# Weight blocks split by DMA: the high part rounded by the loading DMA, the low part accumulated onto its negative

## The chip, the cores and the metric

The kernel runs on one core of one Trainium2 chip. The metric is the device time of one execution in microseconds. Beside the runs that are timed, one execution is profiled; its trace gives the durations used here.

## What is computed

One layer of a hybrid model over 512 tokens of width 2048, in float32. A projection of the input feeds three mixers (retention, mLSTM, an S5 state space with a gated linear unit); their outputs, side by side, go through an output projection, a layer norm, a feed-forward with a squared ReLU, a gate and a second layer norm:

```python
mix = jnp.matmul(jnp.concatenate([y_ret, y_m, y_s], -1), w_out)
x = layer_norm(ALPHA * x + mix, ln1_w, ln1_b)

ff = jnp.matmul(jnp.square(jax.nn.relu(jnp.matmul(x, w_up))), w_down)
r = ALPHA * x + ff
ple = jax.nn.sigmoid(jnp.matmul(r, w_gate)) * jnp.matmul(p_l, w_ple)
return layer_norm(r + ple, ln2_w, ln2_b)
```

`w_up` is 2048 x 8192, `w_down` 8192 x 2048, `w_out` and `w_gate` are 2048 x 2048, `w_ple` is 256 x 2048.

## The kernel before

Activations lie feature-major: a tile of 128 features by 512 tokens. TensorE multiplies in float32r, a float32 with a rounded mantissa. To keep the accuracy of float32, each operand is split into a high part (rounded to float32r) and a low part (the rest), and each product is three matmuls: high by high, high by low, low by high (`mm3`, lines 140 to 143).

All weights are packed on the host into blocks of 128 x 1024 floats (512 KB), in the order in which they are used: W_SU, W_GATE, W_HEAD, W_GLU, then W_OUT (32 blocks), W_PLE (4), W_UP (128), W_DOWN (128) and W_G (32). `wblk` (line 129) fetches one: SP's queue loads it into a tile of the pool with tag "raw" (4 buffers), ScalarE copies it into `wh` (pool "wh", 3 buffers), which rounds it, and VectorE subtracts, `wl = raw - wh` (pool "wl", 3 buffers). These steps have a high priority, so that the scheduler of the program places them early.

The stages from W_OUT on:

- *Output projection.* For 8 groups of two output tiles, 4 blocks each; a block is 24 matmuls of 512 columns.
- *Layer norm and the small projection.* The 16 tiles x1 are normed and split while the 4 blocks of W_PLE are multiplied; the results go to memory.
- *Up and down.* 16 chunks of 512 hidden features. In a chunk, `down` forms seven products for each of two halves (a Strassen scheme with 7 instead of 8), each with a block of W_DOWN or a sum of such blocks; `up` makes the hidden features of the next chunk from 8 blocks of W_UP. Blocks and products alternate: block, product, product, block, and so on. `product` (line 1017) splits its block into `wh` and `wl` of the same two pools as `wblk`, with the same two instructions; its raw blocks have a pool of their own ("rawd").
- *Gate.* 8 groups with 4 blocks of W_G each. Groups 0 to 3 run at full width; groups 4 to 7 run twice, for the first and the second 256 tokens, and load their blocks twice, so that the second layer norm of the first half runs beside the second half's matmuls. So W_G stands for 48 calls of `wblk`.

The pool "wh" and the pool "wl" hand out their buffers in turn, in program order; who takes one waits until TensorE has read what it held before. In the earlier stages POOL's queue carries the S5 part's transfers (lines 400, 401, 478, 567, 568); from the output projection on it has no transfer, and only a third of the last layer norm's tiles (line 114).

Of the kernel before, what the change touches and what calls it, by code (L numbers as in the profile page):

```python
# [10 lines left out]
F32R = mybir.dt.float32r  # L11
# [3 lines left out]
MUL, ADD, SUB, MAX, MIN = ALU.mult, ALU.add, ALU.subtract, ALU.max, ALU.min  # L15
# [58 lines left out]
W_OUT = W_GLU + 2  # L74
# [8 lines left out]
def hybrid_block_kernel(ctx: ExitStack, tc: tile.TileContext, xT, pT, pos, wall, vec, cst, s5b, s5c, out):  # L83
    nc = tc.nc
    V, A, G, P = nc.vector, nc.scalar, nc.gpsimd, nc.tensor

    def pool(name, bufs=1, **kw):
        return ctx.enter_context(tc.tile_pool(name=name, bufs=bufs, **kw))
# [3 lines left out]
    wrp = pool("wr", 4)  # L92
    whp = pool("wh", 3)
    wlp = pool("wl", 3)
# [27 lines left out]
    def acp(out, in_, scale=1.0):  # L122
        return A.activation(out=out, in_=in_, func=AF.Copy, scale=scale)  # L123

    def split(x, hi, lo):
        acp(hi, x)
        pools["dve"] = V.tensor_tensor(out=lo, in0=x, in1=hi, op=SUB).ins  # L127

    def wblk(i, parts=1):
        with tc.high_priority(2000):  # L130
            raw = wrp.tile([128, 1024], F32, tag="raw", name="raw")
            wh = whp.tile([128, 1024], F32R, tag="wh", name="wh")
            wl = wlp.tile([128, 1024], F32R, tag="wl", name="wl")
            for p in range(parts):
                sl = slice(p * 1024 // parts, (p + 1) * 1024 // parts)
                nc.sync.dma_start(out=raw[:, sl], in_=wall[i][:, sl])
                split(raw[:, sl], wh[:, sl], wl[:, sl])
        return wh, wl
# [21 lines left out]
    def gemm(i, banks, acts, m, kb, n=None, sl=slice(0, S)):  # L160
        n = n or KT
        for b in range(n // kb):
            if i == W_SU:
                xload(2 * b)
            wh, wl = wblk(i + b, 2 if i + b == W_SU else 1)
            if i == W_SU:
                xload(2 * b + 1)
            js, qs = range(m), range(kb)
            for j, q in [(j, q) for j in js for q in qs] if n == kb else [(j, q) for q in qs for j in js]:
                k, w = b * kb + q, slice((q * m + j) * 128, (q * m + j + 1) * 128)  # L170
                xh, xl = (a[:, sl] for a in acts[k])
                mm3(banks[j], wh[:, w], wl[:, w], xh, xl, k == 0, k == n - 1)
            tick()
# [745 lines left out]
    for gidx in range(8):  # L919
        tag = ("mm", "bu")[gidx % 2]  # L920
# [18 lines left out]
    for k in range(2):  # L939
        xr = tmp("xr")  # L940
        nc.scalar.dma_start(out=xr, in_=pT[k])
        ph, pl_ = (hfp.tile([128, S], F32R, tag="h" + n, name="p" + n) for n in "hl")
# [28 lines left out]
    def up(c, g, hs):  # L971

        b = [bank("mm"), bank("mm")]
        for i in range(4):
            wh, wl = wblk(W_UP + (2 * c + g) * 4 + i)
            for q in range(4):
                for j in range(2):
                    k, w = 4 * i + q, slice((2 * q + j) * 128, (2 * q + j + 1) * 128)
                    mm3(b[j], wh[:, w], wl[:, w], *x1[k], k == 0, k == KT - 1)
            if i < 3:  # L980
                yield
        for j in range(2):
            r = ffp.tile([128, S], F32, tag="r", bufs=4, name="r")
            with tc.high_priority(400):
                A.activation(out=r, in_=b[j], func=AF.Relu)
                A.activation(out=r, in_=r, func=AF.Square)
            hs.append(r)
        yield
# [135 lines left out]
    def gate_blocks(g, b, i0, i1, sl):  # L1124
        for i in range(i0, i1):
            wh, wl = wblk(W_G + g * 4 + i)
            for q in range(4):
                for j in range(2):
                    k, w = 4 * i + q, slice((2 * q + j) * 128, (2 * q + j + 1) * 128)
                    xh, xl = (a[:, sl] for a in rr[k])  # L1130
                    mm3(b[j], wh[:, w], wl[:, w], xh, xl, k == 0, k == KT - 1)
# [157 lines left out]
```

## Time and profile before

| | |
|---|---|
| median of 3 runs | 2452.59 us (2451.07 to 2454.1) |
| the profiled execution, its own time | 2449.43 us |
| its span, first to last instruction | 2447.6 us |
| mean granted TensorE clock | 0.993 |
| TensorE matmuls busy | 2395.9 us (98%) |
| VectorE, ScalarE, POOL busy | 1816.7, 978.9, 89.4 us |
| transfers | 288.87 MB, mean 118 GB/s |

The stages by time from the span's start: heads until about 660 us, output projection until about 855, layer norm and small projection until about 905, up and down until about 2215, gate until about 2420 (half width from about 2325), the last layer norm to the end. A busy share is an average; what an engine's work is worth is seen in the stretch in which another engine waits for it.

### The profile page before, as it was taken

To read this page: it belongs to the slowest core of one execution; us is meant where nothing else is said; L and a number is where in the kernel's file an instruction comes from. 1 tells how busy PE (TensorE), PEld (TensorE's weight loads), DVE (VectorE), ACT (ScalarE), POOL (GpSimd) and SP (SyncE) were. 2 spreads that over 40 slices of the span, in tenths; PEclk is the share of its full clock that TensorE was granted. 3 is DMA by queue.
4 is the path that set the end of the run, shared out by engine and by line. 5 is a ranking of instruction groups with operands and counts; after the bars stand their busy time and mean duration, and the time that the engine had idled before them with its cause. 6 is when DMAs were issued, how large, how long until landed. Compare 5 with 4: busy or idle time off the path is not lost.

```text
span 2447.6 us, 29501 instructions
## 1 busy us (share of the span) xinstructions
PE 2395.9 (98%) x11123; PEld 1985.3 (81%) x11123; DVE 1816.7 (74%) x2904; ACT 978.9 (40%) x1379; POOL 89.4 (4%) x182
## 2 busy tenths in 40 slices
PE   9999999999999989999999999999999999988996
PEld 7888888888888868888888888888888888867896
DVE  6788989897654476767776777677767776787777
ACT  4544444444432263333433343333334343433354
POOL 4100000000000000000000000000000000000002
PEclk9999999999999999999999999999999999999998
DMA  6433333333443372333333332423242324233464
GB/s 233 146 105 102 110 110 113 113 95 106 155 151 116 117 242 94 100 107 96 111 94 113 93 113 83 124 86 121 78 129 85 117 83 122 85 104 112 129 188 141
DMA packets 99230, 288.87 MB, mean 118 GB/s; under 512 B 11744, under 2 KB 20368, under 8 KB 99088
## 3 DMA queue, kind: packets, MB, share of 16 engines
q1 hardware_dynamic: 85360, 265.49, 34.5%
q10 hardware_dynamic: 8352, 13.11, 1.6%
q0 software_dynamic: 5376, 8.39, 1.3%
q8 instruction: 87, 1.43, 0.2%
q14 instruction: 55, 0.45, 0.1%
HBM read 268.31 MB, written 18.64 MB: 117 GB/s over the span
## 4 chain that ended last, share of the span: by engine, by line
PE 93%; DVE 3%; DMA 1%; issue 1%; ACT 1%; POOL 0%; ACTq 0%; SPq 0%; DVEq 0%
PE mm L141 18%; PE mm L142 18%; PE mm L143 18%; PE wk L1031 13%; PE bu L1031 7%; PE ya L1031 5%; PE bu L142 2%; PE bu L141 2%; PE bu L143 2%; DMA pldr<-t 1%; DVE wl L127 1%; ACT wh L123 1%; PE wk L143 1%; PE wk L142 1%; PE wk L141 1%
## 5 line engine op out<-in xcount | busy, mean ns | idle before, releaser
L123 ACT ACTIVATE wh<-raw 128x1024 fp32r<-128x1024 f32 (+1 forms) x321 | 338.9, 1056 | 739.2 <-PE mm L142 500.7
L127 DVE TENSOR_TENSOR wl<-raw,wh 128x1024 fp32r<-128x1024 f32 (+1 forms) x321 | 391.4, 1219 | 276.0 <-ACT wh L123 267.6
L127 DVE TENSOR_TENSOR wl<-rawd,wh 128x1024 fp32r<-128x1024 f32 x224 | 274.1, 1224 | 179.1 <-ACT wh L123 177.1
L141 PE MATMUL mm<-x1h,wh 128*128 128x512 f32 x1024 | 398.4, 391 | 4.7 <-ACT x1h L123 2.2
L142 PE MATMUL mm<-x1l,wh 128*128 128x512 f32 x1024 | 399.9, 391 | 0.6 <-DVE x1l L127 0.6
L143 PE MATMUL mm<-x1h,wl 128*128 128x512 f32 x1024 | 399.4, 390 | 0.0
L123 ACT ACTIVATE wh<-rawd 128x1024 fp32r<-128x1024 f32 x224 | 237.3, 1060 | 305.5 <-PE wk L1031 210.0
L141 PE MATMUL mm<-xh,wh 128*128 128x512 f32 x800 | 317.4, 397 | 5.3 <-ACT wh L123 5.3
L143 PE MATMUL mm<-xh,wl 128*128 128x512 f32 x800 | 313.1, 391 | 0.0
L142 PE MATMUL mm<-xl,wh 128*128 128x512 f32 x800 | 312.3, 390 | 0.0
L141 PEld LDWEIGHTS mm<-x1h,wh 128*128 128x128 f32 x1024 | 192.3, 188 | 47.8 <-ACT x1h L123 3.5
L142 PEld LDWEIGHTS mm<-x1l,wh 128*128 128x128 f32 x1024 | 192.7, 188 | 42.2 <-DVE x1l L127 1.9
L143 PEld LDWEIGHTS mm<-x1h,wl 128*128 128x128 f32 x1024 | 192.7, 188 | 40.4
L114 DVE TENSOR_TENSOR rawd<-rawd 128x1024 f32<-128x1024 f32 x128 | 156.3, 1221 | 40.7 <-DMA rawd<-in_wall_dram 39.7
L1031 PE MATMUL wk<-wh,fh 128*128 128x512 f32 x448 | 177.5, 396 | 6.5 <-DVE acc L114 6.2
L141 PEld LDWEIGHTS mm<-xh,wh 128*128 128x128 f32 x800 | 150.6, 188 | 34.6 <-ACT wh L123 5.3
L1031 PE MATMUL wk<-wl,fh 128*128 128x512 f32 x448 | 177.1, 395 | 0.0
L143 PEld LDWEIGHTS mm<-xh,wl 128*128 128x128 f32 x800 | 150.4, 188 | 32.0 <-DVE wl L127 0.2
L142 PEld LDWEIGHTS mm<-xl,wh 128*128 128x128 f32 x800 | 150.8, 188 | 29.8
L1031 PE MATMUL wk<-wh,fl 128*128 128x512 f32 x448 | 173.6, 394 | 1.3 <-DVE fl L127 1.3
L114 DVE TENSOR_TENSOR acc<-acc,wk 128x512 f32<-128x512 f32 (+1 forms) x254 | 160.5, 658 | 13.5 <-PE wk L1031 8.3
L1031 PEld LDWEIGHTS wk<-wh,fh 128*128 128x128 f32 x448 | 84.4, 188 | 30.2 <-DVE acc L114 6.2
(433 smaller groups left out, 3903.5 us busy)
## 6 DMA issues: line engine op xcount, KB each, us to landing
raw<-in_wall_dram SPq DMA_DIRECT2D x319, 512.0 KB, 3.7
rawd<-in_wall_dram SPq DMA_DIRECT2D x128, 512.0 KB, 3.6
xr<-in_xT_dram SPq DMA_DIRECT2D x16, 256.0 KB, 4.2
us<-udr POOLq DMA_DIRECT2D x64, 64.0 KB, 2.4
xr<-in_xT_dram ACTq DMA_DIRECT2D x16, 256.0 KB, 3.8
pldr<-t ACTq DMA_DIRECT2D x16, 256.0 KB, 3.2
x1dr<-acc SPq DMA_DIRECT2D x16, 256.0 KB, 2.9
z<-x1dr SPq DMA_DIRECT2D x16, 256.0 KB, 3.3
```

The costliest lines, as they stand in the source:

```text
L114: (e or V).tensor_tensor(out=out, in0=a, in1=b, op=op)
L123: return A.activation(out=out, in_=in_, func=AF.Copy, scale=scale)
L127: pools["dve"] = V.tensor_tensor(out=lo, in0=x, in1=hi, op=SUB).ins
L141: P.matmul(out=ps, lhsT=wh, rhs=xh, start=start, stop=False)
L142: P.matmul(out=ps, lhsT=wh, rhs=xl, start=False, stop=False)
L143: pools["pe"] = P.matmul(out=ps, lhsT=wl, rhs=xh, start=False, stop=stop).ins
L1031: P.matmul(out=banks[t], lhsT=x[:, o], rhs=y[:, w], start=st, stop=x is fl and q == 1, skip_group_check=not first)
```

## The change

In `wblk`, blocks from W_OUT on are fetched in another way. POOL issues a transfer of the block into `wh`, whose type makes the DMA round it to float32r. ScalarE writes `-wh` into `wl`. POOL then issues the same block a second time, as an accumulating transfer onto `wl`, so that `wl = -wh + w`. The tile `raw` goes; `wl` now takes its buffer from the pool of tag "raw" (4 buffers), and `wh` takes its from the pools "wh" and "wl" in turn, by the block's number. VectorE has no part in it. `product` is not changed and takes from both pools as before.

```diff
     def wblk(i, parts=1):
+        if i >= W_OUT:
+
+            with tc.high_priority(2000):
+                pl_, tag = ((whp, "wh"), (wlp, "wl"))[i % 2]
+                wh = pl_.tile([128, 1024], F32R, tag=tag, name="wh")
+                wl = wrp.tile([128, 1024], F32R, tag="raw", name="wl")
+                G.dma_start(out=wh, in_=wall[i])
+                acp(wl, wh, -1.0)
+                G.dma_start(out=wl, in_=wall[i], accum_op=ADD)
+            return wh, wl
         with tc.high_priority(2000):
             raw = wrp.tile([128, 1024], F32, tag="raw", name="raw")
             wh = whp.tile([128, 1024], F32R, tag="wh", name="wh")
```

The order of the engines' instructions, first on ScalarE in an up and down chunk. Before, at the start of a chunk (a copy from `raw` belongs to an up block, one from `rawd` to a product, `fh` is the split of the hidden features):

```order
L123 ACTIVATE fh_9543<-r_9508 128x512
L123 ACTIVATE wh_9638<-raw_9637 128x1024
L123 ACTIVATE fh_9543<-fs_9545 128x1024
L123 ACTIVATE wh_9670<-rawd_9590 128x1024
L123 ACTIVATE wh_9688<-rawd_9594 128x1024
L123 ACTIVATE wh_9707<-raw_9706 128x1024
```

Now, at the same place (the up blocks' step is the one from `wh` to `wl`; the first is block A of the prediction, the second block B):

```order
L123 ACTIVATE fh_9483<-r_9448 128x512
L123 ACTIVATE wh_9608<-rawd_9529 128x1024
L123 ACTIVATE wl_9577<-wh_9576 128x1024
L123 ACTIVATE fh_9483<-fs_9485 128x1024
L123 ACTIVATE wh_9626<-rawd_9533 128x1024
L123 ACTIVATE wl_9645<-wh_9644 128x1024
```

The first product's copy has moved ahead of block A's step; its buffer is the one that the up block before A releases.

On POOL's queue there was nothing here before. Now, in the same chunk, blocks A, B and the next:

```order
L136 DMA wh_9576<-in_wall_dram 128x1024
L138 DMA wl_9577<-in_wall_dram 128x1024
L136 DMA wh_9644<-in_wall_dram 128x1024
L138 DMA wl_9645<-in_wall_dram 128x1024
L136 DMA wh_9710<-in_wall_dram 128x1024
```

Each accumulating load (L138) stands right behind its own rounding load, so the next block's rounding load waits behind it. On POOL's queue in the half-width gate:

```order
L136 DMA wh_18332<-in_wall_dram 128x1024
L138 DMA wl_18278<-in_wall_dram 128x1024
L136 DMA wh_18361<-in_wall_dram 128x1024
L138 DMA wl_18333<-in_wall_dram 128x1024
L136 DMA wh_18390<-in_wall_dram 128x1024
L138 DMA wl_18362<-in_wall_dram 128x1024
```

Here a block's accumulating load stands behind the rounding load of the block after it.

## Rows read from the trace of the kernel before

**Rows 1.** The page, its head and part 1 (TensorE).

```profile
span 2447.6 us, 29501 instructions
PE 2395.9 (98%) x11123; PEld 1985.3 (81%) x11123; DVE 1816.7 (74%) x2904; ACT 978.9 (40%) x1379; POOL 89.4 (4%) x182
```

**Rows 2.** Engines by stretch; the first line names the columns.

```profile
core 0: us, PE busy (x) PEld busy (x) DVE busy (x) ACT busy (x) POOL busy (x), PEclk, DMA share, GB/s
860.00:905.00 45.00, 40.93 (x173) 31.27 (x172) 37.38 (x65) 32.31 (x50) 0.00 (x0) 0.96 0.71 240
905.00:940.00 35.00, 32.94 (x142) 26.08 (x141) 18.31 (x25) 14.45 (x23) 0.00 (x0) 1.00 0.40 136
940.00:2170.00 1230.00, 1229.68 (x5385) 1007.66 (x5383) 898.86 (x1073) 463.09 (x540) 0.00 (x0) 1.00 0.33 103
2170.00:2225.00 55.00, 42.07 (x167) 30.50 (x166) 52.57 (x70) 16.06 (x16) 0.00 (x0) 0.97 0.24 74
2340.00:2395.00 55.00, 54.76 (x455) 54.35 (x455) 42.34 (x79) 30.78 (x49) 8.82 (x9) 1.00 0.67 197
890.00:896.00 6.00, 4.28 (x11) 3.08 (x12) 5.97 (x10) 5.85 (x11) 0.00 (x0) 0.72 0.81 291
2395.00:2447.60 52.60, 28.86 (x227) 28.12 (x225) 35.81 (x84) 22.86 (x45) 10.76 (x12) 0.79 0.41 128
```

**Rows 3.** Timeline of TensorE in the output projection: two matmuls, 24 apart.

```profile
819.69 0.39 PE L141 MATMUL mm<-yh,wh 128*128 128x512 f32 x1
...
825.13 0.39 PE L141 MATMUL mm<-yh,wh 128*128 128x512 f32 x1
```

**Rows 4.** Chain that ended last: the same group of matmuls in two chunks.

```profile
1021.73 2.29 PE bu L1031 x10
...
1103.95 2.29 PE bu L1031 x10
```

**Rows 5.** The page, part 5: the two steps of wblk.

```profile
L123 ACT ACTIVATE wh<-raw 128x1024 fp32r<-128x1024 f32 (+1 forms) x321 | 338.9, 1056 | 739.2 <-PE mm L142 500.7
L127 DVE TENSOR_TENSOR wl<-raw,wh 128x1024 fp32r<-128x1024 f32 (+1 forms) x321 | 391.4, 1219 | 276.0 <-ACT wh L123 267.6
```

**Rows 6.** Groups of VectorE's instructions in 850 to 945.

```profile
L127 DVE TENSOR_TENSOR wl<-raw,wh 128x1024 fp32r<-128x1024 f32 x13 | 15.9, 1224 | 16.8 <-ACT wh L123 16.8
```

**Rows 7.** Tile views: POOL's issue of `us` (ns); landing of `raw`.

```profile
L478 POOL DMA_DIRECT2D us<-udr x64: 489/497/517, 107.2 to 550.2; - x64
...
DMA to landing us min/median/max: 3.3/3.7/6.9
```

**Rows 8.** DMA issues: queue, count, KB each, median us to landing.

```profile
raw<-in_wall_dram SPq DMA_DIRECT2D x319, 512.0 KB, 3.7
...
r<-ydr SPq DMA_DIRECT2D x15, 256.0 KB, 3.6
...
zh<-udr POOLq DMA_DIRECT2D x4, 256.0 KB, 3.0
zl<-udr POOLq DMA_DIRECT2D x4, 256.0 KB, 3.1
```

**Rows 9.** The page, part 3: the queues of SP and of POOL.

```profile
q1 hardware_dynamic: 85360, 265.49, 34.5%
...
q0 software_dynamic: 5376, 8.39, 1.3%
```

**Rows 10.** Timeline of TensorE in the layer norm: a wait.

```profile
889.17 0.39 PE L143 MATMUL mm<-x1h,wl 128*128 128x512 f32 x1
891.73 0.73 PE L141 MATMUL mm<-x1h,wh 128*128 128x512 f32 x2 [2.16 <-ACT x1h L123]
```

## Prediction

> **What bounds the kernel now.** I read the page's busy times first: TensorE is busy 2395.9 of 2447.6 us [rows 1], so a gain can come only from the 52 us in which it is idle. The table of stretches says where those are [rows 2]. In the projection up and down (940 to 2170) TensorE is busy 1229.68 of 1230 us at full clock: whatever VectorE is spared there buys nothing. Idle time lies in 860 to 940 (4.07 and 2.06 us, VectorE busy 37.38 of the first 45), in the last chunk (2170 to 2225: 12.93 us, VectorE busy 52.57 of 55) and in the tail (23.7 us of layer norm). So TensorE's own rate bounds the kernel, and VectorE matters only in two short stretches.
>
> Then I read what a block costs TensorE. In the output projection 24 matmuls go from 819.69 to 825.13, 5.44 us a block [rows 3]. In the up and down loop the same group of matmuls returns one chunk (8 up blocks of 24 and 14 products of 12, 360 matmuls) later after 1103.95 - 1021.73 = 82.22 us [rows 4], 0.2284 us a matmul. In the gate's half-width stretch 455 matmuls take 55 us (the stretch from 2340) [rows 2]: 0.121 us each, 2.90 us a block.
>
> **What is removed.** 212 of the 320 calls of wblk change: 32 of W_OUT, 4 of W_PLE, 128 of W_UP, 48 of W_G (16 at full width, 2 x 16 at half). Each loses one subtraction on VectorE, 1219 ns [rows 5], 258 us in all, and one load on SP's queue. ScalarE keeps one 128x1024 copy per block (1056 ns) [rows 5], now from high part to low. Only where TensorE waits for VectorE can the 258 us count: in 850 to 945 stand 13 of these subtractions, 15.9 us [rows 6], and TensorE's idle time there is 6.1 us plus some 1.7 us of the half-clock dip. I take a gain of 6 us. In the last chunk there are no up blocks; gain 0.
>
> **What is added.** Two loads of 512 KB per block on POOL's queue, in one chain. Before, the raw block was loaded four blocks ahead, and only ScalarE (1.06) and VectorE (1.22) stood between a freed buffer and the matmul. Now the high-part load itself waits for a buffer of the pools "wh" and "wl", shared with the products of down; then come ScalarE's negation, the accumulating load, and the first matmul with wl. The issue on POOL is inside the landing time (0.50 us a load) [rows 7] and two of them fit in any block.
>
> *Landing of a software load.* 256 KB lands in 3.0 and 3.1 us from POOL [rows 8]; 256 KB more at the main queue's mean rate (265.49 MB in 34.5% of 2447.6 us, 314 GB/s) [rows 9] adds 0.83: 3.9 us. The hardware load of 512 KB takes 3.7 [rows 8], so this is near. I charge nothing for software issue, since hardware's 256 KB takes 3.6 us beside software's 3.0 [rows 8]. The Trainium skill says otherwise (DMA: Bandwidth & Descriptors, Specifications: first byte after about 1 us from GpSimd, about 0.6 from SP or ScalarE), a rule against this change; by it a landing would be 4.1 and the sum below some 8 us higher.
>
> *Landing of the accumulating load.* No row shows one. From below it is a plain load, 3.9; from above I take the slowest 512 KB load of this trace, 6.9 [rows 7]. It must read the destination as well as the weights, so I take one more pass of 512 KB: at the best rate of a crowded stretch (291 GB/s at share 0.81, 359 GB/s, the stretch from 890) [rows 2] a pass is 1.46 us: 5.4 us, the lower half of the range. The rounding load I take as a plain one.
>
> *Up and down loop.* Counted in the order listing, between the release and the first matmul with wl lie 49 to 51 matmuls for most up blocks (11.2 to 11.6 us) but 38 for one block in eight (8.68 us). The chain is 0.1 for each of four semaphores + 3.9 + 1.06 + 5.36 = 10.7 us. Most blocks: hidden. The tight one, B: 10.72 - 8.68 = 2.0 us late. The block before it, A, is late in another way: its negation now stands on ScalarE behind a product's copy that waits for the block before, and from there only 25 matmuls (5.71 us) are left: 0.3 + 1.06 + 1.06 + 5.36 = 7.8, 2.1 us late. A and B come in 14 chunks: 14 x 4.1 = 57 us. What queues behind A's negation are the copies of fs and of the next product, which the order still leaves 16 matmuls for; they are about on time.
>
> *Output projection and full-width gate.* A block's low part may be written when block i-4 is done, 75 matmuls ahead: 17 us against 6.8, hidden. Transfers per block: 1.46 + 2.92 + 0.37 (128 KB of inputs) = 4.75, under 5.44: hidden. The cover is 0.7 us; at the upper bound it is gone.
>
> *Half-width gate.* 32 blocks at 2.90 us are 92.8 us, 89.9 up to the last block. At the start 6 high and 4 low buffers may be full. Left are 26 x 1.46 + 28 x 2.92 + 4.2 (other traffic: 197 GB/s over 55 us less 19 blocks, 0.13 us a block [rows 2]) = 124 us of transfers. Here the DMA engines become the bound: +34 us. POOL's additions of the tail stand behind all but the last accumulating load, and that one waits for ScalarE as long.
>
> Sum: 57 + 34 - 6 = +85 us. The profiled execution took 2449.4 us (span 2447.6), 3.2 below the median of 2452.59; so 2534.9 becomes **2538 us**.
>
> **Bounds.** Accumulating load as a plain one: A 0.6 and B 0.6 late, 14 x 1.2 = 17; half-width gate 38 + 41 + 4 = 83, under 89.9, nothing; 17 - 6 = +11, 2464. At 6.9 (4.46 of it transfer): A and B 3.6 each, the six others 0.85 each, 14 x 12.3 = 172; half-width 38 + 125 + 4 = 167, +77; output projection and full gate 6.29 against 5.44, 48 x 0.85 = 41; with -6 together +284, 2736.
>
> **Rivals.**
> 1. *The accumulating load is dear* (about three passes or more, or the rounding load is slow too). Price as above, up to 2736 and beyond. For it: a read-modify-write is a different transfer from every one in this trace. Against: nothing shows it.
> 2. *It is as cheap as a plain load.* 2464, or nearer to no change if the matmul order gives a little.
> 3. *Faster.* If every software load lands in the 3.3 us that is the least a 512 KB load took here [rows 7], A's chain is 0.3 + 2.12 + 3.3 = 5.7 against 5.71 and B's 8.1 against 8.68: no stall in the loop, none in the gate, and the 6 to 8 us of 860 to 940 remain: 2446. The point from which it decides is a landing of 3.3 us. For it: the software loads [rows 8] were no slower than hardware's. Against: the median is 3.7, and traffic on the 16 engines doubles. The Trainium skill (DMA: Bandwidth & Descriptors, Anatomy of one DMA) fits a GpSimd load as 2.0 us plus bytes at 436 GB/s, an estimate of 3.2 us here; by that rule this rival would hold. For 256 KB it gives 2.6, where the trace has 3.0 [rows 8].
> 4. *The clock adds to it.* Before 891.73 TensorE stood still 2.16 us [rows 10], and in 890 to 896 its granted clock was 0.72 [rows 2], 3.4 us at 1.2 GHz, a loss of 1.7. If each of the 28 stalls of 2 us does the same, +47: 2585.
>
> **Chances.** The forecast 36%; with the clock 12%; dear 22%; as cheap as plain 16%; fast landing 11%; 3% for what I don't see. The range leaves out the end of the fast case (5%) and the end of the dear one (some 10%): 2446 to 2736. This kernel's measurements can tell 0.2%, 5 us, from no change. Faster than that: most of case 3, 0.10. Within it: the rest of case 3 and the better half of case 2, 0.13. Slower: 0.77.
>
> **What would show it.** Right: VectorE some 258 us less busy, q0 with some 220 MB more; in 940 to 2170 TensorE idle some 4 us per chunk, in front of matmuls with wl, released by the DMA that writes wl, twice per chunk; in the half-width gate a DMA share near 1 and TensorE waiting for wl; landing of wl about 5.4 us, of wh about 3.9. Wrong: TensorE still at 1229 of 1230 us in the loop (landing of wl below 4), or stalls at every up block and in the output projection (landing of 7 and more), or a clock well below 1 in the loop.

## The result and the profile after

The changed kernel takes 2644.99 us (median of 4 runs, 2635.56 to 2648.5) against 2452.63 us before: a ratio of 1.0778, 95% interval 1.0749 to 1.0808. It is 192 us slower; I had forecast 85. The direction and the range held, the size did not.

The profiled execution has a span of 2645.9 us, 198.3 more than before. Its stages, each from the first to the last of its matmuls, account for that:

| stage | before, us | after, us | difference |
|---|---|---|---|
| output projection | 176.6 | 186.9 | +10.3 |
| small projection, to the first up block | 28.6 | 36.1 | +7.5 |
| first up block to first product | 51.5 | 57.2 | +5.7 |
| first product to last product | 1288.8 | 1407.0 | +118.2 |
| gap, then full-width gate | 102.8 | 105.2 | +2.4 |
| half-width gate | 96.4 | 153.6 | +57.2 |
| rest | 25.7 | 22.5 | -3.2 |

The page of the changed kernel: its span and part 1, two lines of part 3 (queues: packets, MB, share of 16 engines), and part 5 and part 6 where they answer to [rows 1, 5, 7, 8, 9].

```profile
span 2645.9 us, 29679 instructions
...
PE 2458.9 (93%) x11123; PEld 2014.6 (76%) x11123; DVE 1582.0 (60%) x2692; ACT 986.9 (37%) x1379; POOL 388.8 (15%) x606
...
q0 software_dynamic: 66432, 230.72, 39.5%
q1 hardware_dynamic: 54832, 154.33, 17.8%
...
L123 ACT ACTIVATE wl<-wh 128x1024 fp32r<-128x1024 f32 x212 | 224.2, 1058 | 694.7 <-DMA wh<-in_wall_dram 548.6
...
L138 POOL DMA_DIRECT2D wl<-in_wall_dram x212 | 184.4, 872 | 844.8 <-ACT wl L123 749.5
...
L136 POOL DMA_DIRECT2D wh<-in_wall_dram x212 | 127.8, 606 | 843.3 <-PE wk L1041 458.2
...
wh<-in_wall_dram POOLq DMA_DIRECT2D x212, 512.0 KB, 4.8
wl<-in_wall_dram POOLq DMA_DIRECT2D x212, 512.0 KB, 5.6
...
pldr<-t ACTq DMA_DIRECT2D x16, 256.0 KB, 5.7
```

VectorE is 235 us less busy (I had said 258) and the software queue carries 222 MB more [rows 1, 9]: the change does what it says. TensorE's longer busy time is no extra work: the number of matmuls is the same, and some ran at half clock.

The engines by stretch, to be read beside [rows 2]. The stretch from 2312 is the last chunk, that from 2480 lies in the half-width gate.

```profile
core 0: us, PE busy (x) PEld busy (x) DVE busy (x) ACT busy (x) POOL busy (x), PEclk, DMA share, GB/s
860.00:905.00 45.00, 39.09 (x168) 29.84 (x167) 23.08 (x48) 20.75 (x33) 8.05 (x11) 0.92 0.94 253
905.00:940.00 35.00, 26.49 (x96) 19.70 (x95) 18.83 (x30) 22.02 (x34) 5.16 (x7) 0.85 0.93 263
940.00:2170.00 1230.00, 1157.38 (x4925) 933.00 (x4924) 695.65 (x864) 425.40 (x488) 155.33 (x217) 0.98 0.57 139
2312.00:2367.00 55.00, 44.39 (x168) 32.76 (x168) 48.67 (x65) 15.34 (x16) 4.00 (x6) 0.88 0.29 89
2480.00:2600.00 120.00, 86.26 (x614) 81.57 (x613) 21.25 (x66) 39.74 (x59) 38.22 (x54) 0.90 1.01 240
```

In the loop TensorE is idle for 73 us, and its clock is lower too. In the half-width gate the DMA share is 1 at 240 GB/s, where the kernel before had 0.67. What TensorE waited for, over the whole span (time, times, longest):

```profile
engine line waited for: us in total, times, longest us
PE mm L153 <- DMA wl<-in_wall_dram: 92.4, 58, 3.1
PE mm L151 <- ACT t L1175: 18.7, 2, 18.5
PE bu L153 <- DMA wl<-in_wall_dram: 10.0, 8, 2.0
PE mm L151 <- ACT tg L804: 7.2, 1, 7.2
```

The second line is a single wait of 18.5 us in the half-width gate, and what TensorE waits for there is not a load but ScalarE. `t` (L1175) is the step that reads the results of a group of blocks out of TensorE's accumulator `mm` and so frees it:

```profile
2609.10 0.58 PE L151 MATMUL mm<-rh,wh 128*128 128x256 f32 x1 [18.55 <-ACT t L1175]
```

ScalarE is late because from 2554.90 on it has ten negations in a row, each of which waits for its rounding load; the last two, and behind them the layer norm of the first 256 tokens (L1197, L907):

```profile
2594.16 1.06 ACT L123 ACTIVATE wl<-wh 128x1024 fp32r<-128x1024 f32 x1 [3.95 <-DMA wh<-in_wall_dram]
2597.93 1.06 ACT L123 ACTIVATE wl<-wh 128x1024 fp32r<-128x1024 f32 x1 [2.71 <-DMA wh<-in_wall_dram]
2598.89 0.55 ACT L1197 ACTIVATE xr<-wk,vv 128x256 f32<-128x256 f32 x1
```

VectorE, whose part of that layer norm needs ScalarE's `q`, stands still as long (times as above: in all, how often, longest):

```profile
DVE acc L111 <- ACT q L907: 66.4, 11, 46.9
```

Blocks A and B of one chunk can be followed through three engines. ScalarE first (start, duration, and in brackets the idle time before it and its releaser):

```profile
1315.76 1.07 ACT L123 ACTIVATE wh<-rawd 128x1024 fp32r<-128x1024 f32 x1 [3.21 <-PE mm L152]
1316.73 1.04 ACT L123 ACTIVATE wl<-wh 128x1024 fp32r<-128x1024 f32 x1
...
1332.44 1.06 ACT L123 ACTIVATE wl<-wh 128x1024 fp32r<-128x1024 f32 x1 [12.64 <-DMA wh<-in_wall_dram]
```

POOL's queue, A's two loads and B's:

```profile
1311.13 0.57 POOL L136 DMA_DIRECT2D wh<-in_wall_dram  x1 [5.18 <-issue]
1318.06 0.86 POOL L138 DMA_DIRECT2D wl<-in_wall_dram  x1 [6.37 <-DVE fl L127]
1328.59 0.57 POOL L136 DMA_DIRECT2D wh<-in_wall_dram  x1 [9.67 <-PE wk L1041]
1333.79 0.86 POOL L138 DMA_DIRECT2D wl<-in_wall_dram  x1 [4.63 <-ACT wl L123]
```

And TensorE, at A and then at B:

```profile
1321.06 0.40 PE L152 MATMUL mm<-x1l,wh 128*128 128x512 f32 x1
1323.68 0.79 PE L153 MATMUL mm<-x1h,wl 128*128 128x512 f32 x1 [2.23 <-DMA wl<-in_wall_dram]
1324.28 0.63 PE L151 MATMUL mm<-x1h,wh 128*128 128x512 f32 x1
1324.70 0.63 PE L152 MATMUL mm<-x1l,wh 128*128 128x512 f32 x1
...
1339.04 0.50 PE L153 MATMUL mm<-x1h,wl 128*128 128x512 f32 x1 [2.09 <-DMA wl<-in_wall_dram]
```

At A the negation (1316.73) stands behind the product's copy, which TensorE released after 3.21 us; the accumulating load goes out at 1318.06 and TensorE continues at 1323.68. At B it is the rounding load that waited 9.67 us for a product's buffer. Behind A the matmuls are 0.43 us apart instead of 0.228: the granted clock is at 1.2 GHz for 3.4 us.

Over the 14 chunks, the first matmul with wl comes late by a median of 2.23 us at A and 2.47 at B (32.2 and 34.9 us in all), at the other blocks by 18.7 us in all. Behind 13 of the 28 stalls at A and B the clock is at 1.2 GHz for 3.4 us, 44.4 us in all; half of that, 22.2, is lost. Together 108.0 of the loop's 118.2. Another 4.7 us are in the last chunk, which has no up blocks; its clock is low for 13.7 us, where before it was for 3.4. The remaining 5.5 are not assigned.

### The profile page after: what moved, and what is told of

It reads as the page before. It is cut to its first block, busy times and chain, and to the rows that moved or that the text cites. A ratio compares the mean times of both kernels' runs of the same rounds, so it can differ in the third digit from the quotient of the medians.

```text
span 2645.9 us, 29679 instructions
## 1 busy us (share of the span) xinstructions
PE 2458.9 (93%) x11123; PEld 2014.6 (76%) x11123; DVE 1582.0 (60%) x2692; ACT 986.9 (37%) x1379; POOL 388.8 (15%) x606
## 3 DMA queue, kind: packets, MB, share of 16 engines
q0 software_dynamic: 66432, 230.72, 39.5%
q1 hardware_dynamic: 54832, 154.33, 17.8%
## 4 chain that ended last, share of the span: by engine, by line
issue 48%; PE 34%; POOL 7%; DMA 5%; DVE 3%; ACT 1%; POOLq 0%; ACTq 0%; SPq 0%; DVEq 0%
PE mm L153 8%; PE mm L151 8%; PE mm L152 8%; POOL wl L138 4%; DMA wh<-in_wall_dram 4%; POOL wh L136 3%; PE bu L151 1%; PE bu L152 1%; PE bu L153 1%; PE wk L1041 1%; DMA wl<-in_wall_dram 1%; ACT wl L123 1%; PE wk L153 1%; DVE acc L114 1%; PE wk L151 1%
## 5 line engine op out<-in xcount | busy, mean ns | idle before, releaser
L153 PE MATMUL mm<-x1h,wl 128*128 128x512 f32 x1024 | 414.8, 405 | 77.3 <-DMA wl<-in_wall_dram 76.9
L123 ACT ACTIVATE wl<-wh 128x1024 fp32r<-128x1024 f32 x212 | 224.2, 1058 | 694.7 <-DMA wh<-in_wall_dram 548.6
L151 PE MATMUL mm<-x1h,wh 128*128 128x512 f32 x1024 | 408.1, 400 | 8.5 <-ACT r L995 5.3
L152 PE MATMUL mm<-x1l,wh 128*128 128x512 f32 x1024 | 407.8, 398 | 0.0
L127 DVE TENSOR_TENSOR wl<-rawd,wh 128x1024 fp32r<-128x1024 f32 x224 | 274.1, 1224 | 92.0 <-ACT wh L123 46.5
L138 POOL DMA_DIRECT2D wl<-in_wall_dram x212 | 184.4, 872 | 844.8 <-ACT wl L123 749.5
L136 POOL DMA_DIRECT2D wh<-in_wall_dram x212 | 127.8, 606 | 843.3 <-PE wk L1041 458.2
L114 DVE TENSOR_TENSOR acc<-acc,ya 128x512 f32<-128x512 f32 x92 | 63.2, 687 | 267.7 <-PE ya L1041 267.5
L123 ACT ACTIVATE wh<-raw 128x1024 fp32r<-128x1024 f32 (+1 forms) x109 | 114.3, 1049 | 185.5 <-PE mm L152 120.1
```

The source lines that it names most:

```text
L114: (e or V).tensor_tensor(out=out, in0=a, in1=b, op=op)
L136: G.dma_start(out=wh, in_=wall[i])
L138: G.dma_start(out=wl, in_=wall[i], accum_op=ADD)
L151: P.matmul(out=ps, lhsT=wh, rhs=xh, start=start, stop=False)
L152: P.matmul(out=ps, lhsT=wh, rhs=xl, start=False, stop=False)
L153: pools["pe"] = P.matmul(out=ps, lhsT=wl, rhs=xh, start=False, stop=stop).ins
```

## The experiments

**Theory:** the loop loses to the chain of rounding load, negation and accumulating load behind shared buffers at A and B, and to the clock behind those stalls; the half-width gate to full DMA engines; the stretch before the loop to crowded transfers. **Rivals:** the traffic or POOL's serial queue itself, whatever the buffers; a latency chain and not the DMA engines in the gate; two loads a block, whatever their kind. The wait for ScalarE in the gate, shown above, was not among them, and no experiment was made for it; what the traces of the others say of it stands with e3 and e8.

### Buffers of their own for the up blocks (e1)

```diff
+                if W_UP <= i < W_DOWN:
+                    pl_, tag = wrp, "raw"
                 wh = pl_.tile([128, 1024], F32R, tag=tag, name="wh")
```

> Only the up blocks change: both of their tiles now come from the four buffers of the pool with tag raw, so the rounding load no longer waits for a product's buffer (64 or more matmuls lie between the release and the first use, before 39 to 51, and 51 or more behind the negation, before 26 at block A). Theory, that the loop loses time to the chain of rounding load, negation and accumulating load behind shared buffers at blocks A and B, and to the clock that falls behind those two stalls: 51 matmuls are 11.6 us against a chain of 10.7, so the stalls and the dips of the clock in the loop go, the loop falls from 1407 to about 1290 to 1300 us, the whole to 2527 to 2540. Rival, that the doubled traffic or POOL's serial queue makes the loads late whatever the buffers: the loop stays above 1380, the whole above 2615.

2544.71 us, 1.0379 of before (1.0363 to 1.0394). Once the loop runs, no stall is left, with both dear loads still in it:

```profile
1300.00:2170.00 870.00, 869.86 (x3820) 716.80 (x3819) 541.85 (x683) 334.27 (x385) 122.19 (x171) 1.00 0.60 154
```

TensorE is busy 869.86 of 870 us at full clock, DMA share 0.60. So neither the traffic nor POOL's queue was the loop's loss; the buffers were. First to last product takes 1309.0 us, not 1407.0. The 20 left over lie at its start: between 906 and 986 TensorE waits for wl at nine of the first up blocks, 19.6 us in all. I take it that two blocks in flight are too few there; e13, whose first eight blocks go the old way, has no such wait. My figure of 2527 to 2540 was 5 us too low for that reason.

### The negation on VectorE (e2)

```diff
-                acp(wl, wh, -1.0)
+                (ts(wl, wh, -1.0, None, MUL) if W_UP <= i < W_DOWN else acp(wl, wh, -1.0))
```

> Only the negation of the up blocks moves from ScalarE to VectorE, so that it doesn't stand behind a product's copy. Theory: block A is no longer late (its rounding load is 50 matmuls ahead, 11.4 us against 10.7), block B stays (37 matmuls, 8.45 us): one stall of about 2 us and one dip of the clock fewer in each of 14 chunks, 14 x 4 = 56 us, the whole 2580 to 2600. If A's stall came from its loads and not from the place of its negation: no change, 2640 or more. If the stalls at other blocks are caused by the same loads: also no change there.

2647.61 us, 1.0786 (1.0766 to 1.0806): no gain, and my figure missed. A's lateness falls from 32.2 to 20.0 us in all, B's rises from 34.9 to 46.4. A's new rest is a new queue: in one chunk A's high part landed at 1325.58 and VectorE negated it at 1326.81, behind a product's subtraction. B has 36 matmuls ahead instead of 38, and from its rounding load's issue to that of its accumulating load pass 5.85 us, where it was 5.20:

```profile
1337.22 0.57 POOL L136 DMA_DIRECT2D wh<-in_wall_dram  x1 [8.56 <-issue]
1343.07 0.86 POOL L138 DMA_DIRECT2D wl<-in_wall_dram  x1 [5.28 <-DVE wl L118]
```

The place of the negation does set part of A's stall, but moving one link of a chain between shared buffers handed the time to the next block.

### The second load without accumulation (e3)

```diff
-                G.dma_start(out=wl, in_=wall[i], accum_op=ADD)
+                G.dma_start(out=wl, in_=wall[i])
```

> Leaves out the accumulation: the second load writes the rounded block onto wl instead of adding to the negated high part, so the low part of the weights is wrong and the rest of the work is the same, the load's wait for the negation too. Theory, that the accumulating load's own duration (landing 5.4 against 3.9, and 328 against 174 ns a packet on the DMA engines) sets the size: in the loop A and B are 0.6 us late or less, the loop at 1295 to 1325 instead of 1407; in the half-width gate two loads take 2 x 8 packets x 0.174 = 2.8 us of each engine, 3.2 with other traffic, against 2.9 of matmuls: about 105 us instead of 154; the output projection back to 177. The whole 2475 to 2530. Rival, that it is the number of software loads or the wait for the negation and not the accumulation: the half-width gate stays above 135 and the loop above 1380, the whole above 2600.

2550.85 us, 1.0399 (1.0384 to 1.0415). The loop falls to 1338.6 us, the half-width gate to 126.9, both between the two theories. So of the 192 us, 94 hang on the accumulation and 98 remain with two loads that only round, the negation between them and the shared buffers. In the half-width gate the wait for ScalarE remains (17.8 us in one piece): the last load lands 109 us after the stage's start, near the 105 of the theory, and the stage ends at 126.9. Landings over the run:

```profile
wh<-in_wall_dram POOLq DMA_DIRECT2D x212, 512.0 KB, 4.4
wl<-in_wall_dram POOLq DMA_DIRECT2D x212, 512.0 KB, 3.9
```

At B a median lateness of 1.82 us remains (A 0.49): there the rounding load counts, and it is longer than I took it. In the gate, 105 us of this kernel give the price of a rounding load on full engines:

```profile
q0 software_dynamic: 7651, 27.82, 82.5%
```

27.82 MB are 53.1 loads; in 0.825 x 105 us that is 1.63 us of all 16 engines each; I had 1.46. (Counting the 50 loads that were issued in the stretch I first took 1.73, which the expectation of e8 uses.) The same line of the changed kernel, 2480 to 2600:

```profile
q0 software_dynamic: 7433, 27.10, 95.8%
```

That is 51.7 loads in 115.0 us, 4.45 for a pair; less 1.63, an accumulating load takes 2.8 us, if half of the bytes are of each kind; I had 2.92. So the pair costs 4.45 us where I had 4.38.

### More buffers in the half-width gate (e4)

```diff
+                if i >= W_G + 16:
+                    wl = rp_.tile([128, 1024], F32R, tag="wg", bufs=10, name="wl")
```

> Only the half-width gate's low parts change: ten buffers of their own instead of the four with tag raw. Theory, that the 16 DMA engines are full there: the half-width gate stays at 4.8 us a block, less what ten buffers may have filled ahead, the whole 2630 to 2647. Rival, that the chain (release, negation, accumulating load) behind four buffers sets it: the half-width gate falls from 154 to 115 us or less, the whole to 2605 or less.

2658.72 us, 1.0849 (1.083 to 1.0868), above my 2630 to 2647: the half-width gate takes 162.7 us, not less but 9 more. POOL's queue now sends up to three rounding loads in a row,

```profile
2560.05 1.96 POOL L139 DMA_DIRECT2D wh<-in_wall_dram  x3
```

and they land after 8.4 to 11.7 us: more in flight only wait longer. That speaks for the DMA engines and against the latency chain, as far as the loads go; the wait for ScalarE is here too (19.0 us). The loss itself may come from the new pool, which opens later, so that fewer blocks are loaded ahead; this I did not test alone.

### One stage at a time (e5, e6, e7)

```diff
-        if i >= W_OUT:
+        if W_UP <= i < W_DOWN:
```

This is e5; in e6 the condition is `i >= W_G`, in e7 `W_OUT <= i < W_UP`.

> The new path for the 128 up blocks alone, the old one for all others. Theory, that each stage loses by itself: the loop's +118 us and some of the 13 us before it (its first blocks are fetched during the layer norm), nothing in the output projection and in the gate: 2565 to 2585. Rival, that the loop's stalls need the other stages' loads, or that the early loss is the up blocks' own: below 2550, or above 2590.

> The new path for the gate's 48 calls alone. Theory: +57 in the half-width gate, where the 16 DMA engines are full, +6 in the full-width gate, -4 at its start: 2500 to 2520, with the loop at 1289 as before. Rival, that the gate was slow because it was entered late or with empty buffers after the loop's stalls: half-width gate below 140, the whole below 2490.

> The new path for the 32 blocks of the output projection and the 4 of the small projection alone. Theory, that the burst of the first loads delays the loads of r that ScalarE waits for (one stall of 7 us and a dip of the clock) and that crowded engines delay the small projection's results: +10 in the output projection, +3 to +13 after it: 2463 to 2477. Rival, that the loss there came from the first up blocks' loads only: 2450 to 2460.

- e5: 2597.56 us, 1.0598 (1.0567 to 1.0629), +146. More than I said, and in the range of the rival: in its profiled execution, the slowest of the four, the loop takes 1426.9 us, with 68.3 us at 1.2 GHz, and the stretch from the end of the output projection to the first product takes 96.7 us instead of 80.1. So the early loss arises with the up blocks' first loads alone.
- e6: 2513.24 us, 1.026 (1.0241 to 1.028), +61, as expected; the half-width gate 155.1 us, the loop 1291.3.
- e7: 2460.68 us, 1.0038 (1.0023 to 1.0053), +9. The output projection's +11 is there alone, and it is one stall, with 6.8 us at 1.2 GHz behind it:

```profile
PE mm L151 <- ACT tg L804: 7.3, 1, 7.3
```

The sum of the three is 216, the whole 192: they are separate but for some 24 us; in the profiled executions the up blocks cost less in the full change than alone (loop and early stretch together 131 against 155 us). What e7 lost it keeps up to the first product (+13.6); only +9.7 is left in its span at the end.

The stall of e7 is also in the changed kernel, at 685.69. The loads of r that the first matmuls need share the engines with ten weight loads sent ahead and land after 5.9 us instead of 3.6; ScalarE, which splits r, stands behind them, and with it the copy (tg) that frees TensorE's accumulator.

### Half of the change (e8)

```diff
+                nc.sync.dma_start(out=raw, in_=wall[i])
+                G.dma_start(out=wh, in_=wall[i])
+                pools["dve"] = V.tensor_tensor(out=wl, in0=raw, in1=wh, op=SUB).ins
```

> Half of the change alone: SP loads the raw block, POOL's transfer rounds the high part, VectorE subtracts as before; nothing accumulates. It has as many transfers as the change. Theory, that the accumulating transfer is the dear part: 24 to 26 matmuls (5.5 to 5.9 us) lie ahead of the first use, the chain is 3.9 + 0.2 + 1.22 = 5.3, so the loop has small stalls at most, 1289 to 1310; in the half-width gate 1.46 + 1.73 us of all engines a block, 3.3 with the rest, against 2.9: +13; the whole 2455 to 2490. Rival, that two transfers a block are what costs, whatever their kind: half-width gate above 130, the whole above 2520.

2516.55 us, 1.0266 (1.0251 to 1.0282). The loop takes 1316.1 us and the half-width gate 120.9, in which the engines are nearly full without any accumulation:

```profile
2375.00:2480.00 105.00, 90.19 (x666) 86.41 (x665) 65.26 (x118) 20.23 (x48) 25.00 (x37) 0.93 0.93 305
```

My 2455 to 2490 was too low: two transfers a block cost some 65 us without accumulation, without the negation and with the old buffers. The other 127 of the 192 hang on these three together. In this kernel ScalarE has no step in fetching a block, and the wait for it in the gate is not there.

### The output projection without its start (e9)

```diff
-        if i >= W_OUT:
+        if W_OUT + 8 <= i < W_PLE:
```

> The new path for W_OUT's blocks from the ninth on alone; the first eight and all later blocks by the old path. Theory, that the output projection's +10 us is the burst at its start (up to ten weight loads ahead of the loads of r) and the +13 behind it the crowding of the layer norm's transfers by new-path loads: both go, and the blocks in the steady state are hidden: 2447 to 2457, no change. Rival, that the steady state costs too (the engines are busy 4.8 of 5.44 us a block): 2460 or more.

2456.88 us, 1.0014 (1.0005 to 1.0022). The stall is gone, and so is the loss behind it. 24 blocks by the new path in the steady state cost 1 to 5 us by the interval; in the profiled execution the output projection takes 177.1 us instead of 176.6, so they are all but hidden, as the prediction's step had it.

### VectorE relieved by POOL (e10, e11, e12)

```diff
-                split(raw[:, sl], wh[:, sl], wl[:, sl])
+                acp(wh[:, sl], raw[:, sl])
+                tt(wl[:, sl], raw[:, sl], wh[:, sl], SUB, G)
```

These are the kernel before with subtractions moved to POOL: in e10 those of the small projection and the first eight up blocks; in e11 those of the gate's first four blocks and of eight results; in e12 also the differences of weight blocks in the last chunk.

> The kernel before, with the subtraction of the four blocks of the small projection and the first eight up blocks on POOL instead of VectorE: the relief of VectorE in 850 to 945 without a second load. Theory, that VectorE's 15.9 us there are worth the 6 us that I took as gain: 2446 to 2450. Rival, that ScalarE's copies and not VectorE set that stretch, or that POOL's slower subtraction is late: 2452 or more.

> The kernel before, with the subtraction of the gate's first four blocks and of the eight results of the last chunk on POOL. VectorE is busy 52.57 of the last chunk's 55 us and TensorE idle 12.93; 6.3 us of VectorE's work leave: 2445 to 2450 if VectorE's order of work allows it; no change if its first half, where TensorE waits for the products' own split, is what counts.

> As the run before, and the five differences of weight blocks in each half of the last chunk on POOL too, 8.5 us off VectorE in the last chunk. A difference on POOL takes some 3 us by the nearest rows (2.0 and 2.9 us for 128x1088) against 1.22: 2441 to 2449 if POOL keeps ahead of the products (2.74 us each), 2455 or more if a product waits for it.

2460.42 us (1.0026, 1.0016 to 1.0036), 2451.15 (0.9996, 0.9987 to 1.0005) and 2457.82 (1.0017, 1.0009 to 1.0026): no gain anywhere, and in e10 and e12 a small loss. In e10 VectorE's other work became slower meanwhile. Its split of x1, 860 to 940, before and in e10, and POOL's subtraction in e10:

```profile
L127 DVE TENSOR_TENSOR x1l<-acc,x1h 128x512 fp32r<-128x512 f32 x16 | 11.0, 686 | 0.9 <-ACT x1h L123 0.7
...
L127 DVE TENSOR_TENSOR x1l<-acc,x1h 128x512 fp32r<-128x512 f32 x16 | 16.6, 1037 | 4.2 <-ACT x1h L123 4.1
...
L114 POOL TENSOR_TENSOR wl<-raw,wh 128x1024 fp32r<-128x1024 f32 x12 | 28.8, 2404 | 296.1 <-ACT wh L123 296.1
```

1037 ns each instead of 686. So e10 does not settle what VectorE's relief alone is worth there.

### Own buffers in the loop alone, and the gate's full width alone (e13, e14)

```diff
-        if i >= W_OUT:
+        if W_UP + 8 <= i < W_DOWN:
```

This is e13, on top of e1's edit; e14 is the changed kernel with `W_G <= i < W_G + 16`.

> The new path with both tiles from the pool with tag raw, for the up blocks from the ninth on alone; all others by the old path. Theory, that the shared buffers were all of the loop's loss: 120 blocks by the dear path cost nothing, 2449 to 2459, with VectorE some 146 us less busy. Rival, that the doubled traffic in the loop costs time by itself, whatever the buffers (the 20 us left over in e1): 2465 or more.

> The new path for the 16 full-width blocks of the gate alone. Theory, that a block of 5.44 us of matmuls covers 4.8 us of the engines, but not the burst of the first blocks, which have no loads ahead: +2 to +8, 2455 to 2461, and the half-width gate at 96 as before. Rival, that full width is hidden altogether and the loss at the start came from the half-width loads behind it: 2449 to 2454.

e13: **2445.61 us, 0.9972 (0.9961 to 0.9982): 0.3% faster than the kernel before.** 120 blocks by the dear path cost nothing with buffers of their own, so the shared buffers were all of the loop's loss from the ninth block on. The small gain I had not expected. e14: 2461.16 us, 1.0032 (1.0019 to 1.0044); the full-width stage takes 105.2 us instead of 98.9 and starts without the gap before it. Gap and full width together cost 2.4 us, as in the changed kernel. The half-width gate takes 98.6 us, 2.2 more than before; but it takes 98.4 in e16, whose gate is the old one. Its profiled execution is 13.7 us longer than that of before, 3.7 of it ahead of the first up block, which the edit does not touch, and 3.7 in the last chunk. So the stage explains 2.4 of the 9 us by which the median rose; the rest I can't explain.

### Where e13's gain is (e15, e16, e17)

```diff
-        if W_UP + 8 <= i < W_DOWN:
+        if W_UP + 112 <= i < W_DOWN:
```

This is e15; in e16 the condition is `W_UP + 8 <= i < W_UP + 112`.

> The path of e13 for the last 16 up blocks alone. Theory, that the gain is made where the loop runs into its last chunk, in which TensorE waits for VectorE and ScalarE: the whole gain remains, 2444 to 2448. Rival, that it needs the relief over the whole loop: 2450 to 2455.

> The path of e13 for the up blocks from the ninth to the 112th. Theory: no gain is left, 2450 to 2456, as TensorE was busy 1229.68 of 1230 us there before. Rival, that the relief counts anywhere in the loop: 2444 to 2448.

e15: 2452.6 us, 1.0001 (0.9993 to 1.001). e16: 2446.07 us, 0.9979 (0.997 to 0.9988). My theory of the last chunk fell: the gain is in every chunk. A chunk takes 82.0 us in e13 and e16 and 82.2 in e15 and before, 0.22 us x 13 = 3; another 1.5 us comes between the first up block and the first product, and in e13 2.6 us in the last two chunks. (The profiled execution of e16 is the slowest of its eleven, 2451.62 us; it shows the shorter chunks, but not the gain in the whole.) The stretch from 1100 to 1920, first of the kernel before, then of e13:

```profile
1100.00:1920.00 820.00, 820.00 (x3593) 672.38 (x3592) 600.43 (x718) 307.22 (x358) 0.00 (x0) 1.00 0.33 103
```

```profile
1100.00:1920.00 820.00, 820.00 (x3603) 676.18 (x3602) 510.19 (x641) 314.21 (x361) 114.71 (x161) 1.00 0.61 154
```

TensorE counts as busy all the time in both, and does 3593 matmuls in one and 3603 in the other. Where the difference sits is seen at its weight loads (PEld) in the same stretch of the kernel before. The columns are as in the table of waits:

```profile
PEld wk L1031 <- DVE fl L127: 2.4, 10, 0.3
PEld wk L1031 <- ACT fh L123: 2.1, 10, 0.2
```

Twice in each of the ten chunks a product's weight load waits some 0.2 us, for `fl`, VectorE's split of the hidden features, and for `fh`, which ScalarE makes from VectorE's `fs`. The matmuls before are still counted as running, so the busy time shows no gap; but their starts, 0.228 us apart elsewhere, are 0.27 and 0.30 apart there, and with some smaller delays around them this makes the 0.22 us. In e13 no weight load waits in this stretch. Last, e17 gives VectorE work again in e13:

```diff
+                junk = ffp.tile([128, 256], F32, tag="junk", bufs=1, name="junk")
+                for h in range(3):
+                    tt(junk, wh[:, h * 256:h * 256 + 256], wh[:, 768:], SUB)
                 acp(wl, wh, -1.0)
```

> e13 with three subtractions of 128x256 on VectorE for each of its 120 blocks, into a tile that nothing reads, some 1.3 us a block as the subtraction that e13 took away (1.22). If VectorE's relief makes the gain: 2450 to 2456, a chunk at 82.2 us. If the buffers and the order make it: 2443 to 2448, a chunk at 82.0.

2451.62 us, 0.9997 (0.9988 to 1.0006): the gain is gone, its best chunks are at 82.2 us again, and the wait for VectorE's split is back:

```profile
PEld bu L1046 <- DVE fl L127: 6.1, 10, 1.3
```

That points to VectorE's relief and not to the buffers. It is not clean: the added work waits for the load in VectorE's queue and delays what stands behind it, and TensorE is idle 2.7 us in the same stretch, which it was not in e13.

## Why the prediction was right and wrong

The mechanism that I put into the sum was there, but the sum was less than half of what was measured. Four of its steps failed. The loop, 57, measured 118: I put the lower clock behind the stalls and the lateness of the other blocks at nothing. The half-width gate, 34, measured 57: I had a head start that was not there, and the wait for ScalarE was missing. The gain of 6 us around the layer norm was a loss of 13. And the start of the output projection, which I called hidden, cost 10.

- **Landings and the stalls at A and B: right.** In a quiet part of the loop wh mostly lands in 3.8 to 4.3 us (forecast 3.9), wl in 5.2 to 5.6 (5.36). A and B are late by 2.23 and 2.47 us where I had 2.1 and 2.0: 67 us for 57. e1 and e13 show that the cause is the one named. The third rival, a landing of 3.3 us, is refuted, and with it the fit of the Trainium skill (DMA: Bandwidth & Descriptors, Anatomy of one DMA) for these loads: an estimate of 3.2 us by it, medians of 4.8 and 5.6 here.
- **The clock: a rival that I should have put into the sum.** I kept the forecast free of it though [rows 10] showed the dip behind a stall of 2.16 us. It took 22 us behind A and B. The rival's price of 47 was too high: of the 28 stalls at A and B only 13 are followed by a dip; the one at 1339.04 is not. Why the others are not stays open.
- **The other up blocks "hidden": nearly.** They add 18.7 us in all; my chain of 10.7 against 11.2 us left little room for loads that are slower than the median.
- **"I take a gain of 6 us" in 860 to 940: the step that failed in sign.** From the end of the output projection to the first product the kernel lost 13 us. VectorE was relieved as I said (41.91 us busy of 80 against 55.68), but the DMA share rose to 0.93, the stores of the small projection land after 5.7 us instead of 2.1, and ScalarE, which needs their buffers, waited 16.8 us for them in 860 to 905, where it had waited 7.6:

```profile
ACT t L123 <- DMA pldr<-t: 16.8, 7, 4.0
```

  How much of the 13 us this wait makes was not tested alone. e5 has the loss without new loads for the small projection itself.

- **Output projection hidden: right in its steady state (e9), wrong at its start.** I counted its own blocks and not whom their first ten loads delay: +10 us.
- **Half-width gate bound by the DMA engines: right for the loads, but not the whole.** Forecast +34, measured +57. The price of a block was right: 4.45 us of all engines, where I had 4.38. The head start of 6 high and 4 low parts was smaller: when the stage begins at 2469.7, four high and two low parts are loaded. The last low part lands at 2606.9, 137 us after the start, where my sum had 124. With one block's matmuls behind it (2.9 us) the stage would have ended after 140 us; it took 153.6. The other 13 to 14 us are the wait for ScalarE: the layer norm of the first half, which was to run beside the second half's matmuls, stood in ScalarE's queue behind negations that waited for loads, and the step that frees the accumulator stood behind it. My sum looked at POOL's additions of the tail and not at ScalarE. The wait is in the profiled executions of all kernels with the new path in the half-width gate (e1, e2, e3, e4, e6: 15.8 to 19.0 us) and not in e8; no edit moved the negation alone there. e4 speaks against the latency chain for the loads.
- **"Whatever VectorE is spared there buys nothing": wrong by some 5 us.** e13 and e16 gain 0.2 to 0.3% in a loop in which TensorE counts as busy 99.97% of the time; the waits of its weight loads for VectorE's split are what the busy time hid. The Trainium skill has the warning (Trainium Kernel Development and Optimization, Best Practices: distance to the peak is not judged by the busy share of the matmuls), and the two rows of 820.00 us agree.

In sum: forecast 57 - 6 + 34 = 85. Measured by the same steps in the profiled execution: 67 at A and B, 19 at other blocks, 22 by the clock behind A and B and 5 in the last chunk (with 5 unassigned, 118); 57 in the half-width gate, of which 13 to 14 by ScalarE; 13 instead of -6 around the layer norm; 10 at the start of the output projection; the rest about zero.

## What to carry to other kernels

A load that moves from "four blocks ahead into a buffer of its own" to "behind a shared buffer, in a chain with another load" is no longer a prefetch: count the matmuls between the release and the first use for every position, then add the lower clock that follows a stall. Price added traffic where the DMA engines are fullest and by whom it delays (small stores and loads of others), not only by its own consumer; over the whole span the two queues' shares of 39.5% and 17.8% hid stretches at 0.9 and 1. A step that waits for a load holds up all that stands behind it in its engine's queue: ask what that is, as here a layer norm and the freeing of an accumulator. And an engine that counts as 100% busy can still do a little more: look at the waits of its weight loads.

## What the runs showed of the hardware that was not expected

- On full DMA engines a 512 KB load of 4 KB packets takes 1.63 us of all 16 when it rounds (e3), and about 2.8 when it accumulates. A 4 KB packet takes a median of 159 ns in a plain load and 174 in a rounding one, side by side in e8 (2375 to 2480), and 327 in the changed kernel's accumulating ones.
- Issuing an accumulating load occupies POOL for 872 ns, a rounding one for 606.
- A 128x1024 subtraction takes 2404 ns on POOL and 1224 on VectorE, and slows VectorE's beside it from 686 to 1037 ns for 128x512 (e10). The Trainium skill names a shared port of the two engines (Trainium Architecture — The Big Picture, What this means for kernel authors), as an exclusive lock; the longer mean agrees with contention, but no run here tells a lock from a shared rate.
